# A hybrid decoder trunk in exact halves: one matmul over both halves of x in the MLP and the dilated q, k

## The chip, the cores and the metric

The kernel runs on one core of one Trainium2 chip. The metric is the device time of one execution in microseconds. A core has TensorE (PE, the matmuls; PEld is its loading of the stationary operand), VectorE (DVE), ScalarE (ACT), GpSimd (POOL) and SyncE (SP, which here issues the DMAs). The engines run their own queues in order and wait for one another on semaphores.

## What is computed

Four layers over a residual stream of 256 tokens by 1024 features, in float32. Each layer has a token mixer (a convolution module, dilated attention, RWKV-7, a convolution module), a cross-attention into 256 memory tokens, and an MLP with a squared ReLU; after each of them stands a LayerNorm.

```python
def sq_relu_mlp(x, w1, w2):
    return jnp.square(jax.nn.relu(x @ w1)) @ w2

def dilated_attention(x, w_qkv, w_out, rel_bias):
    qkv = (x @ w_qkv).reshape(b, s, n_groups, 3, DIL_HEADS, DIL_HEAD_DIM)
    for g, (win, dil) in enumerate(DIL_GROUPS):     # three groups, 16 heads of 64
        o, lse = dilated_group_attention(qkv[:, :, g, 0], qkv[:, :, g, 1], qkv[:, :, g, 2], win, dil, rel_bias)
        ...
    wts = jax.nn.softmax(jnp.stack(lses), axis=0)
    o = jnp.einsum('gbsh,gbshe->bshe', wts, jnp.stack(outs))
    return o.reshape(b, s, DIL_HEADS * DIL_HEAD_DIM).astype(x.dtype) @ w_out

def reference(x, mem, ...):
    for i in range(DEPTH):                          # 4
        h = ...                                     # conv, dilated, rwkv7, conv
        x = layer_norm(DEEPNORM_ALPHA * x + h, ln_g[i, 0], ln_b[i, 0])
        h = memory_cross_attention(x, mem, x_w_q[i], x_w_kv[i], x_w_out[i])
        x = layer_norm(DEEPNORM_ALPHA * x + h, ln_g[i, 1], ln_b[i, 1])
        h = sq_relu_mlp(x, m_w1[i], m_w2[i])        # 1024 -> 4096 -> 1024
        x = layer_norm(DEEPNORM_ALPHA * x + h, ln_g[i, 2], ln_b[i, 2])
```

## The kernel before

**Exact halves.** Every matrix product with weights is made from numbers cut in two. A number's high half is its value rounded to float32r, the low half is the rest. A product is then three matmuls into the same sum: high weights with high x, high weights with low x, low weights with high x.

**Weights.** `chunk` (L129) streams 512 KB at a time: a DMA into one of three `ws` buffers, a cast on ACT to the high half `wh` (L137), a subtraction to the low half `wl` (L138) on DVE, in places on POOL. `wh` and `wl` have nine buffers each, so a cast waits until the matmuls have finished with the chunk nine places back.

**x.** Both halves of x, transposed (features on partitions, eight blocks of 128 features, 256 tokens), lie in two tiles, `xth` and `xtl`, made by `split` (cast on ACT L151, subtraction on DVE L152).

**PSUM** has eight banks of 512 columns in three rings: A (four), B (two) and T (two, for transposes).

**MLP** (`mlp`, L399). The 4096 hidden columns are 16 units of 256. The first four are made by `first_units`; for the other twelve, `up(u)` makes a unit's hidden block with its features on partitions: `gemm_feat` runs over two halves c of 128 columns and eight blocks k of x, three matmuls of 256 tokens each (L181), 48 in all, into one bank of ring B. ACT applies Relu (L417) and Square (L418), and `split` leaves the halves `hth`, `htl`. `down(u, t)` multiplies a hidden block with its rows of w2 by `gemm_tok` (L169, 512 columns), 12 matmuls per token tile, into four A banks that are held for the whole MLP. Steps of `down(u, 0)`, `down(u, 1)`, `up(u + 5)` alternate.

**Dilated attention** (`dilated`). For each of eight pairs of heads (hp), three groups g, and q and k, `qk_unit` streams one chunk and makes 24 matmuls of 256 columns (L644) into one bank of ring B. ACT takes the sum out to the tile `qk`, scaled for q (L647), copied for k (L649). `v_units` makes the values (L193). `scores(h)` of a head makes the scores of the second token tile (L693, s1 in two A banks) and of the first (L695, s0 in a B bank); the softmax on DVE adds the biases (L673) out of PSUM, ACT takes the exponential (L679). `flip` transposes the result (L708, copies L710), `values` multiplies it with the values (L720). Scores, transposes and values of a pair are set between the next pair's `qk_unit` steps by the loop at the end of `dilated`.

**Order.** The kernel's code gives each instruction a place. A scheduler of the framework then makes one static order for each engine. At run time each engine's queue runs in that order.

**Other tiles that the change touches.** Keys and values of the cross-attention (`kv_alloc`: `kt`, `vt`, two buffers each), the memory's halves (`mem_t`), the biases and scores of the dilated attention (`hks`, `sbs`), and RWKV's `XV` and `rW` share the rings `kt`, `vt`, `xth`, `xtl`.

Of the kernel before, what the change touches and what calls it, by code (L numbers as in the profile page):

```python
# [19 lines left out]
P = 128  # L20
# [52 lines left out]
def merge(tracks):  # L73
    """Emits the steps of (generator, rank) tracks by rank; a step yields how far its track's rank moves on."""
# [9 lines left out]
class Trunk:  # L84
# [25 lines left out]
    # ---- tiles  # L110
# [61 lines left out]
    def gemm_feat(self, xt, unit, ps, toks=slice(0, S)):  # L172
        """ps[:, c, toks] = (x @ w).T of the unit's 256 columns, feature major."""
        nc = self.nc
        xh, xl = xt[0][:, :, toks], xt[1][:, :, toks]
        for c in range(2):
            for k in range(KC):
                hi, lo = unit[k // 4]
                a, b = hi[:, k % 4, c * P:(c + 1) * P], lo[:, k % 4, c * P:(c + 1) * P]
                for i, (l, r) in enumerate(((a, xh[:, k, :]), (a, xl[:, k, :]), (b, xh[:, k, :]))):  # L180
                    nc.tensor.matmul(ps[:, c * S + toks.start:c * S + toks.stop], l, r, start=k == 0 and i == 0,  # L181
                                     stop=k == KC - 1 and i == 2)
# [1162 lines left out]
```

## Time and profile before

| | |
|---|---|
| time, median of 3 executions | 2081.34 us (2080.61 to 2085.47) |
| span of the profiled execution | 2084.1 us |
| DVE busy | 1316.5 us (63%) |
| ACT busy | 998.0 us (48%) |
| POOL busy | 265.6 us (13%) |
| read from HBM | 318.81 MB, 156 GB/s over the span with the writes |
| L181: matmuls of `gemm_feat` | 3 x 1280 of 128x256 |
| L644: matmuls of `qk_unit` | 3 x 384 of 128x256 |

The profile is of one execution; no time beside its span is given for it. It lies 2.8 us above the median, within the range of the three times. The rows of a timeline give an instruction's start, its duration, engine, line, operation, tiles and shapes, and in brackets how long its engine had been idle and what released it. Rows of groups give a count, the busy time and the mean duration in ns. Durations of matmuls overlap, so the time that a matmul takes in a stream is the distance between two starts.

The page's rows of 40 slices show that PE is the busy engine nearly everywhere, with its granted clock high:

```profile
PE   7999999999999999999989989989999888999998
DVE  3986674564555557654496578777644499667454
ACT  4546455544444435455436543334645355645552
```

### The profile page before, as it was taken

To read this page: it belongs to the slowest core of one execution; us is meant where nothing else is said; L and a number is where in the kernel's file an instruction comes from. 1 tells how busy PE (TensorE), PEld (TensorE's weight loads), DVE (VectorE), ACT (ScalarE), POOL (GpSimd) and SP (SyncE) were. 2 spreads that over 40 slices of the span, in tenths; PEclk is the share of its full clock that TensorE was granted. 3 is DMA by queue.
4 is the path that set the end of the run, shared out by engine and by line. 5 is a ranking of instruction groups with operands and counts; after the bars stand their busy time and mean duration, and the time that the engine had idled before them with its cause. 6 is when DMAs were issued, how large, how long until landed. Compare 5 with 4: busy or idle time off the path is not lost.

```text
span 2084.1 us, 34386 instructions
## 1 busy us (share of the span) xinstructions
PE 1975.3 (95%) x13717; PEld 1781.3 (85%) x13717; DVE 1316.5 (63%) x2516; ACT 998.0 (48%) x1548; POOL 265.6 (13%) x160
## 2 busy tenths in 40 slices
PE   7999999999999999999989989989999888999998
PEld 7998889978989988899889878778898787888996
DVE  3986674564555557654496578777644499667454
ACT  4546455544444435455436543334645355645552
POOL 6860000000000000000021221100000663000000
PEclk8999999999999999999999989989999999999999
DMA  7644466557666635466636343433766441446652
GB/s 225 193 154 141 144 191 193 182 165 181 161 150 146 165 86 182 151 201 186 195 121 218 91 130 100 121 122 115 223 189 188 157 152 49 134 142 193 191 183 80
DMA packets 284992, 327.93 MB, mean 157 GB/s; under 512 B 25333, under 2 KB 253437, under 8 KB 284832
## 3 DMA queue, kind: packets, MB, share of 16 engines
q1 hardware_dynamic: 284832, 325.75, 52.0%
q8 instruction: 107, 1.75, 0.3%
q14 instruction: 53, 0.43, 0.1%
HBM read 318.81 MB, written 6.89 MB: 156 GB/s over the span
## 4 chain that ended last, share of the span: by engine, by line
PE 64%; DVE 14%; DMA 10%; ACT 6%; issue 3%; POOL 2%; SPq 0%; ACTq 0%; DVEq 0%; POOLq 0%
PE psA L169 20%; PE psB L181 18%; PE psB L644 6%; PE psB L193 4%; ACT wh L137 3%; DVE wl L138 3%; DVE g L535 3%; DMA ws<-in_m_w_dram 3%; PE psT L217 2%; PE psA L209 2%; POOL wl L138 2%; PE psA L193 2%; DMA ws<-in_x_w_kv_dram 2%; PE psB L370 1%; DVE bnst L267 1%
## 5 line engine op out<-in xcount | busy, mean ns | idle before, releaser
L137 ACT CAST wh<-ws 128x1024 fp32r<-128x1024 f32 x546 | 572.7, 1050 | 737.2 <-PE psA L169 197.1
L138 DVE TENSOR_TENSOR wl<-ws,wh 128x1024 fp32r<-128x1024 f32 (+1 forms) x462 | 569.5, 1234 | 415.5 <-ACT wh L137 410.9
L181 PE MATMUL psB<-xth,wh 128*128 128x256 f32 x1280 | 368.2, 288 | 8.6 <-ACT xth L151 3.6
L181 PE MATMUL psB<-xth,wl 128*128 128x256 f32 x1280 | 366.5, 286 | 7.7 <-DVE wl L138 7.7
L181 PE MATMUL psB<-xtl,wh 128*128 128x256 f32 x1280 | 367.0, 287 | 0.0
L181 PEld LDWEIGHTS psB<-xth,wh 128*128 128x128 f32 x1280 | 249.3, 195 | 12.9 <-ACT xth L151 3.8
L138 POOL TENSOR_TENSOR wl<-ws,wh 128x1024 fp32r<-128x1024 f32 x84 | 210.7, 2527 | 385.0 <-DMA ws<-in_a_w_in_dram 273.0
L181 PEld LDWEIGHTS psB<-xth,wl 128*128 128x128 f32 x1280 | 249.2, 195 | 8.9 <-DVE wl L138 8.6
L181 PEld LDWEIGHTS psB<-xtl,wh 128*128 128x128 f32 x1280 | 249.4, 195 | 2.3 <-issue 0.2
L169 PE MATMUL psA<-wh,hth 128*128 128x512 f32 x512 | 163.7, 396 | 0.0
L169 PE MATMUL psA<-wh,htl 128*128 128x512 f32 x512 | 163.3, 395 | 0.0
L169 PE MATMUL psA<-wl,hth 128*128 128x512 f32 x512 | 162.2, 393 | 0.0
L209 PE MATMUL psA<-wh,xth 128*128 128x256 f32 x512 | 145.7, 285 | 0.0
L209 PE MATMUL psA<-wh,xtl 128*128 128x256 f32 x512 | 145.4, 287 | 0.2 <-DVE xtl L152 0.2
L209 PE MATMUL psA<-wl,xth 128*128 128x256 f32 x512 | 144.5, 283 | 0.0
L535 DVE SCALAR_TENSOR_TENSOR psA<-chp,ccols,psA 128x256 f32<-128x256 f32 x280 | 119.1, 482 | 3.0 <-PE psA L519 0.4
L644 PE MATMUL psB<-xth,wh 128*128 128x256 f32 x384 | 112.6, 293 | 6.4 <-ACT qk L647 4.6
L169 PEld LDWEIGHTS psA<-wl,hth 128*128 128x128 f32 x512 | 96.5, 188 | 22.9
L169 PEld LDWEIGHTS psA<-wh,htl 128*128 128x128 f32 x512 | 96.2, 188 | 22.0
L844 POOL MEMSET rH<- 128x512 f32 x1 | 0.5, 527 | 894.0 <-DVE bnst L267 894.0
L644 PE MATMUL psB<-xtl,wh 128*128 128x256 f32 x384 | 110.5, 288 | 0.0
L644 PE MATMUL psB<-xth,wl 128*128 128x256 f32 x384 | 110.1, 287 | 0.0
(327 smaller groups left out, 3994.3 us busy)
## 6 DMA issues: line engine op xcount, KB each, us to landing
ws<-in_m_w_dram SPq DMA_DIRECT2D x256, 512.0 KB, 3.8
ws<-in_b_w_qkv_dram SPq DMA_DIRECT2D x72, 512.0 KB, 3.8
ws<-in_x_w_kv_dram SPq DMA_DIRECT2D x64, 512.0 KB, 3.6
ws<-in_a_w_in_dram SPq DMA_DIRECT2D x32, 512.0 KB, 4.5
ws<-in_x_w_q_dram SPq DMA_DIRECT2D x32, 512.0 KB, 4.3
ws<-in_x_w_out_dram SPq DMA_DIRECT2D x32, 512.0 KB, 3.9
ws<-in_c_w_rkv_dram SPq DMA_DIRECT2D x24, 512.0 KB, 4.4
ws<-in_a_w_out_dram SPq DMA_DIRECT2D x16, 512.0 KB, 3.3
```

The source lines that it names most:

```text
L137: nc.scalar.copy(out=h[:rows], in_=f[:rows])
L138: self.lo_eng.tensor_tensor(l[:rows], f[:rows], h.bitcast(F32)[:rows], op=OP.subtract)
L169: nc.tensor.matmul(ps[j], l, r[:, j * 512:(j + 1) * 512], start=first and k == 0 and i == 0, stop=last and k == n - 1 and i == 2)
L181: nc.tensor.matmul(ps[:, c * S + toks.start:c * S + toks.stop], l, r, start=k == 0 and i == 0, stop=k == KC - 1 and i == 2)
L193: nc.tensor.matmul(ps[:, m * 256:(m + 1) * 256], l, r[:, k % 4, :], start=k == 0 and i == 0, stop=k == KC - 1 and i == 2)
L209: nc.tensor.matmul(out[-1][:, o], l, r[:, k % 4, :], start=k == 0 and i == 0, stop=k == KC - 1 and i == 2)
L217: self.pe_last = self.nc.tensor.transpose(pt[:, i * P:(i + 1) * P], b, self.ident).ins
L267: v.bn_stats(st[:, j, :], xs)
L370: nc.tensor.matmul(op[:, c * S:(c + 1) * S], vt[:, m, (2 * h + c) * P:(2 * h + c + 1) * P], pT[:, m, :], start=m == 0, stop=m == 1)
L535: v.scalar_tensor_tensor(dst[:, o], hp[:, c, k:k + S], dwc(k, cc), src[:, o], op0=OP.mult, op1=OP.add)
L644: nc.tensor.matmul(ps, l[:, k, :], r[:, k, :], start=k == 0 and i == 0, stop=k == KC - 1 and i == 2)
L844: nc.gpsimd.memset(H, 0.0)
```

## The change

1. **One tile for both halves of x.** `halves` allocates x's high and low parts in one tile, [128, 8, 2, 256], so that for each block k the 512 columns [high | low] are contiguous.
2. **`feat2`** replaces `gemm_feat` in the MLP's `up` and the three matmuls in `qk_unit`. For each block k it makes one matmul of 512 columns with the high weights, over both halves of x, into a whole bank of ring B, and one of 256 columns with the low weights and high x, into the left half of that bank. Three matmuls and three weight loads become two and two. In the MLP each half c of a unit has a bank of its own.
3. **The eviction** adds the bank's halves: ACT copies (or scales) the right half to SBUF, DVE adds the left half to it (in `qk_unit` with q's scale). In the MLP Relu then reads SBUF.
4. **Rings.** `xth` and `xtl` become one ring `xt`, `kt` and `vt` one ring `kv`, with two buffers each; all tiles in them are merged pairs. RWKV's W of both token tiles is one tile. Comments are removed, and line numbers move.

`gemm_feat` stays for the cross-attention, the convolutions and RWKV.

```diff
+    def halves(self, tag, name):
+        x = self.sb.tile([P, KC, 2, S], F32R, name=name, tag=tag, bufs=2)
+        return x[:, :, 0, :], x[:, :, 1, :], x
+
     def xt(self):
-        h = self.sb.tile([P, KC, S], F32R, name="xth", tag="xth", bufs=2)
-        l = self.sb.tile([P, KC, S], F32R, name="xtl", tag="xtl", bufs=2)
-        return h, l
+        return self.halves("xt", "xt")
...
+    def feat2(self, xt, w):
+        nc = self.nc
+        ps = self.B()
+        for k in range(KC):
+            a, b = w(k)
+            nc.tensor.matmul(ps, a, xt[2][:, k].rearrange("p a b -> p (a b)"), start=k == 0, stop=k == KC - 1,
+                             skip_group_check=True)
+            nc.tensor.matmul(ps[:, :S], b, xt[0][:, k, :], start=False, stop=k == KC - 1, skip_group_check=True)
+        return ps
...
     def kv_alloc(self):
-        kt = self.sb.tile([P, KC, S], F32, name="kt", tag="kt", bufs=2)
-        vt = self.sb.tile([P, NT, D], F32, name="vt", tag="vt", bufs=2)
-        return kt, vt
+        kv = self.sb.tile([P, 2, 2048], F32, name="kv", tag="kv", bufs=2)
+        return kv[:, 0].rearrange("p (a b) -> p a b", b=S), kv[:, 1].rearrange("p (a b) -> p a b", b=D)
...
         def up(u):
-            ps = self.B()
-            self.gemm_feat(xt, self.colunit(w1, u * 256), ps)
+            unit = self.colunit(w1, u * 256)
             r = self.g2()
-            nc.scalar.activation(r, ps, AF.Relu)
+            for c in range(2):
+                ps = self.feat2(xt, lambda k: [a[:, k % 4, c * P:(c + 1) * P] for a in unit[k // 4]])
+                o = r[:, c * S:(c + 1) * S]
+                nc.scalar.copy(out=o, in_=ps[:, S:])
+                nc.vector.tensor_tensor(o, o, ps[:, :S], op=OP.add)
+            nc.scalar.activation(r, r, AF.Relu)
             nc.scalar.activation(r, r, AF.Square)
             self.split(*hidden(u), r.rearrange("p (a b) -> p a b", a=2))
...
-        hks = self.sb.tile([P, 2, 4, S], F32, name="hks", tag="kt", bufs=2)
-        sbs = self.sb.tile([P, 2, 1024], F32, name="sbs", tag="vt", bufs=2)
+        hs = self.sb.tile([P, 2, 2, 1024], F32, name="hs", tag="kv", bufs=2)
+        hks, sbs = hs[:, 0].rearrange("p a (b c) -> p a b c", c=S), hs[:, 1]
...
         def qk_unit(hp, g, c):
-            ps = self.B()[:, :S]
-            for k in range(KC):
-                for i, (l, r) in enumerate(((hi, xt[0]), (hi, xt[1]), (lo, xt[0]))):
-                    nc.tensor.matmul(ps, l[:, k, :], r[:, k, :], start=k == 0 and i == 0, stop=k == KC - 1 and i == 2)
+            ps = self.feat2(xt, lambda k: (hi[:, k, :], lo[:, k, :]))
             o = qk[hp, g, c] = dp.tile([P, S], F32, name="qk", bufs=12)
-            if c == 0:
-                nc.scalar.mul(out=o, in_=ps, mul=DE ** -0.5)
-            else:
-                nc.scalar.copy(out=o, in_=ps)
+            sc = DE ** -0.5 if c == 0 else 1.0
+            nc.scalar.mul(out=o, in_=ps[:, S:], mul=sc)
+            v.scalar_tensor_tensor(o, ps[:, :S], sc, o, op0=OP.mult, op1=OP.add)
...
-            W = st["W", t] = self.sb.tile([P, NH, 2, 2, P], F32, name="rW", bufs=2,
-                                            tag=(("kt", "vt") if hq != 2 else ("xth", "xtl"))[t])
+            if t == 0:
+                st["WW"] = self.sb.tile([P, NT, NH, 2, 2, P], F32, name="rW", bufs=2, tag="kv" if hq != 2 else "xt")
+            W = st["W", t] = st["WW"][:, t]
```

**Where the instructions stand.** In the MLP, on PE at the beginning of a unit: the last matmuls of a down product (psA), then the first of the unit (psB). Before:

```order
L169 MATMUL psA_3283<-wh_3360,htl_3030 128x512
L169 MATMUL psA_3284<-wh_3360,htl_3030 128x512
L181 MATMUL psB_3389<-xth_2338,wh_3391 128x256
L181 MATMUL psB_3389<-xtl_2339,wh_3391 128x256
L181 MATMUL psB_3389<-xth_2338,wl_3392 128x256
```

and of the changed kernel, on the same engine at the same place:

```order
L172 MATMUL psA_3274<-wh_3340,htl_3021 128x512
L172 MATMUL psA_3275<-wh_3340,htl_3021 128x512
L195 MATMUL psB_3382<-xt_2332,wh_3370 128x512
L197 MATMUL psB_3382<-xt_2332,wl_3371 128x256
L195 MATMUL psB_3382<-xt_2332,wh_3370 128x512
```

The unit keeps its place between the down products; three matmuls of a block have become two.

In the dilated attention, on PE around the scores of an even head, whose newest k has just been made (in the trace near 580.8 us). Before:

```order
L644 MATMUL psB_5920<-xth_2972,wl_5916 128x256
L708 MATMUL psT_5982<-ident_72,sbs_4787 128x128 x2
L693 MATMUL psA_5949<-qk_5945,qk_5912 128x256
L695 MATMUL psB_5950<-qk_5669,qk_5607 128x128
L695 MATMUL psB_5950<-qk_5816,qk_5783 128x128
L695 MATMUL psB_5950<-qk_5945,qk_5912 128x128
L693 MATMUL psA_6076<-qk_5669,qk_5607 128x256
L693 MATMUL psA_6076<-qk_5816,qk_5783 128x256
L644 MATMUL psB_6000<-xth_2972,wh_5995 128x256
```

and of the changed kernel, where the scores have the lines L708 (before L693) and L710 (before L695):

```order
L195 MATMUL psB_5657<-xt_2964,wh_5652 128x512
L197 MATMUL psB_5657<-xt_2964,wl_5653 128x256
L708 MATMUL psA_5679<-qk_5674,qk_5648 128x256
L710 MATMUL psB_5680<-qk_5426,qk_5371 128x128
L710 MATMUL psB_5680<-qk_5559,qk_5533 128x128
L710 MATMUL psB_5680<-qk_5674,qk_5648 128x128
L708 MATMUL psA_5792<-qk_5426,qk_5371 128x256
L708 MATMUL psA_5792<-qk_5559,qk_5533 128x256
L195 MATMUL psB_5730<-xt_2964,wh_5725 128x512
```

The scores with the newest k, qk_5674, now follow its unit directly; the two transposes have moved ahead of the unit.

On DVE at the same place, before (wl are weights' low halves for later units, dmx and sbs belong to the softmax of these scores):

```order
L673 ISA sbs_4787,dmx_5958<-psA_5948,hks_4786 128x512
L673 ISA dmx_5958 128x1
L138 TENSOR_TENSOR wl_6309<-ws_6307,wh_6308 128x1024
L138 TENSOR_TENSOR wl_6381<-ws_6379,wh_6380 128x1024
L673 ISA sbs_4787,dmx_5960<-psA_5949,hks_4786,dmx_5958 128x256
```

and of the changed kernel, where L664 is the new addition to qk, and the subtraction's line is L141:

```order
L688 ISA hs_4644,dmx_5688<-psA_5678,hs_4644 128x512
L688 ISA dmx_5688 128x1
L664 SCALAR_TENSOR_TENSOR qk_5648<-psB_5631,qk_5648 128x256
L141 TENSOR_TENSOR wl_5997<-ws_5995,wh_5996 128x1024
L141 TENSOR_TENSOR wl_6069<-ws_6067,wh_6068 128x1024
L664 SCALAR_TENSOR_TENSOR qk_5674<-psB_5657,qk_5674 128x256
L688 ISA hs_4644,dmx_5690<-psA_5679,hs_4644,dmx_5688 128x256
```

The addition that completes the newest k, qk_5674, stands behind two weight subtractions, the second of which (wl_6069) has the place of wl_6381 before. On ACT the cast of that chunk stands ahead of the copy of qk in both kernels.

More of the change, by code (lines that the diff above doesn't have):

```diff
@@ L157, in gemm_tok @@
         nc = self.nc
-        xh, xl = xt
+        xh, xl = xt[:2]
         n = len(ws)
@@ L170, in gemm_tok, with gemm_feat, feat @@
                                      start=first and k == 0 and i == 0, stop=last and k == n - 1 and i == 2)
-    def gemm_feat(self, xt, unit, ps, toks=slice(0, S)):
+    def gemm_feat(self, xt, unit, ps):
+        for c in range(2):
+            self.feat(ps[:, c * S:(c + 1) * S], xt, lambda k: [a[:, k % 4, c * P:(c + 1) * P] for a in unit[k // 4]])
+    def feat(self, ps, xt, w):
         nc = self.nc
-        xh, xl = xt[0][:, :, toks], xt[1][:, :, toks]
-        for c in range(2):
-            for k in range(KC):
[L178 to L182, printed above, removed]
+        for k in range(KC):
+            a, b = w(k)
+            for i, (l, r) in enumerate(((a, xt[0]), (a, xt[1]), (b, xt[0]))):
+                nc.tensor.matmul(ps, l, r[:, k, :], start=k == 0 and i == 0, stop=k == KC - 1 and i == 2)
+    def feat2(self, xt, w):
+        nc = self.nc
+        ps = self.B()
+        for k in range(KC):
+            a, b = w(k)
+            nc.tensor.matmul(ps, a, xt[2][:, k].rearrange("p a b -> p (a b)"), start=k == 0, stop=k == KC - 1,
+                             skip_group_check=True)
+            nc.tensor.matmul(ps[:, :S], b, xt[0][:, k, :], start=False, stop=k == KC - 1, skip_group_check=True)
+        return ps
     def gemm_unit(self, xt, unit, ps, tiles=(0, 1)):
         nc = self.nc
-        xh, xl = xt
+        xh, xl = xt[:2]
         for m in tiles:
@@ L198, in first_units @@
         nc = self.nc
-        xh, xl = xt
+        xh, xl = xt[:2]
         out = []
@@ L220, in to_xt @@
     def to_xt(self, xt, src, t):
-        xh, xl = xt
+        xh, xl = xt[:2]
         for q in range(2):
@@ L289, in mem_t @@
         if spare:
-            mt = (self.sb.tile([P, KC, S], F32R, name="mth", tag="kt", bufs=2),
-                  self.sb.tile([P, KC, S], F32R, name="mtl", tag="vt", bufs=2))
+            mt = self.halves("kv", "mt")
         elif pool is None:
@@ L294, in mem_t @@
         else:
-            mt = pool.tile([P, KC, S], F32R, name="mth"), pool.tile([P, KC, S], F32R, name="mtl")
+            mt = pool.tile([P, KC, 2, S], F32R, name="mt")
+            mt = mt[:, :, 0, :], mt[:, :, 1, :], mt
         for m in range(NT):
@@ L413, in up @@
         def up(u):
-            ps = self.B()
-            self.gemm_feat(xt, self.colunit(w1, u * 256), ps)
+            unit = self.colunit(w1, u * 256)
             r = self.g2()
-            nc.scalar.activation(r, ps, AF.Relu)
+            for c in range(2):
+                ps = self.feat2(xt, lambda k: [a[:, k % 4, c * P:(c + 1) * P] for a in unit[k // 4]])
[3 more added lines that the diff above has]
+            nc.scalar.activation(r, r, AF.Relu)
             nc.scalar.activation(r, r, AF.Square)
@@ L612, in dil_table @@
         nc.sync.dma_start(rb[:BUCKETS, :], t_["rel_bias"])
-        oh = self.sb.tile([P, G, TW], F32, name="onehot", tag="kt", bufs=2)
+        oh = self.sb.tile([P, G, TW], F32, name="onehot", tag="kv", bufs=2)
         nc.sync.dma_start(oh[:BUCKETS + 1], t_["rel_onehot"])
@@ L640, in qk_unit @@
             hi, lo = self.chunk(w[:, c0:c0 + P].rearrange("(k p) n -> p k n", p=P), (KC, P))
-            ps = self.B()[:, :S]
-            for k in range(KC):
-                for i, (l, r) in enumerate(((hi, xt[0]), (hi, xt[1]), (lo, xt[0]))):
-                    nc.tensor.matmul(ps, l[:, k, :], r[:, k, :], start=k == 0 and i == 0, stop=k == KC - 1 and i == 2)
+            ps = self.feat2(xt, lambda k: (hi[:, k, :], lo[:, k, :]))
             o = qk[hp, g, c] = dp.tile([P, S], F32, name="qk", bufs=12)
-            if c == 0:
-                nc.scalar.mul(out=o, in_=ps, mul=DE ** -0.5)
-            else:
-                nc.scalar.copy(out=o, in_=ps)
+            sc = DE ** -0.5 if c == 0 else 1.0
+            nc.scalar.mul(out=o, in_=ps[:, S:], mul=sc)
+            v.scalar_tensor_tensor(o, ps[:, :S], sc, o, op0=OP.mult, op1=OP.add)
         def v_units(hq, gs):
@@ L816, in rwkv @@
         XK, XR = self.xt(), self.xt()
-        XV = (self.sb.tile([P, KC, S], F32R, name="xvh", tag="kt", bufs=2),
-              self.sb.tile([P, KC, S], F32R, name="xvl", tag="vt", bufs=2))
+        XV = self.halves("kv", "xv")
         def mixes(m, dst):
```

## The prediction

> **What bounds the kernel now.** I read the page's busy lines first, then its chain, then a table of stretches.
>
> ```profile
> span 2084.1 us, 34386 instructions
> ...
> PE 1975.3 (95%) x13717; PEld 1781.3 (85%) x13717; DVE 1316.5 (63%) x2516; ACT 998.0 (48%) x1548; POOL 265.6 (13%) x160
> ...
> PE 64%; DVE 14%; DMA 10%; ACT 6%; issue 3%; POOL 2%; SPq 0%; ACTq 0%; DVEq 0%; POOLq 0%
> PE psA L169 20%; PE psB L181 18%; PE psB L644 6%; PE psB L193 4%; ACT wh L137 3%; DVE wl L138 3%; DVE g L535 3%; DMA ws<-in_m_w_dram 3%; PE psT L217 2%; PE psA L209 2%; POOL wl L138 2%; PE psA L193 2%; DMA ws<-in_x_w_kv_dram 2%; PE psB L370 1%; DVE bnst L267 1%
> ```
>
> TensorE is busy 95% of the span, and the two lines that the change rewrites, L181 and L644, hold 24% of the chain that ended last. The stretches to look at are one MLP (308 to 433 us) and the dilated attention (487 to 755 us).
>
> ```profile
> 308.00:433.00 125.00, 125.00 (x796) 113.31 (x795) 62.72 (x56) 66.78 (x80) 0.00 (x0) 1.00 0.61 190
> 487.00:755.00 268.00, 258.11 (x2028) 242.57 (x2027) 138.36 (x269) 120.51 (x202) 0.00 (x0) 0.98 0.64 160
> ```
>
> The columns are the stretch, its length, busy time of PE, PEld, DVE, ACT and POOL with counts, granted clock, DMA share and GB/s. In the MLP PE never pauses (125.00 of 125.00, clock 1.00), while DVE and ACT work half of the time and the DMA engines 0.61. There a shorter PE stream shortens the stretch, and DVE and ACT have room. The dilated stretch already has 9.9 us without matmuls: there PE sometimes waits for others.
>
> **The matmuls saved.** A matmul's recorded duration overlaps its successor, so I count the time from start to start.
>
> ```profile
> 351.23 0.28 PE L181 MATMUL psB<-xtl,wh 128*128 128x256 f32 x1
> ...
> 352.43 0.28 PE L181 MATMUL psB<-xth,wl 128*128 128x256 f32 x1
> 352.55 0.62 PE L169 MATMUL psA<-wh,hth 128*128 128x512 f32 x2
> ...
> 355.33 0.64 PE L169 MATMUL psA<-wh,hth 128*128 128x512 f32 x2
> ...
> 262.67 0.62 PE L169 MATMUL psA<-wl,xth 128*128 128x512 f32 x2
> ...
> 267.65 0.61 PE L169 MATMUL psA<-wh,xth 128*128 128x512 f32 x2
> ```
>
> From 351.23 to 352.43 ten 256-column matmuls of the MLP start: 120 ns each (119.8 over the stretch). Of 512 columns, six pairs from 352.55 to 355.33 give 232 ns each, and eleven pairs of a projection, from 262.67 to 267.65, give 226 to 227. So two 256-column matmuls cost 239.6, one of 512 columns 227 to 232: the join saves 12.6 ns, or 7.5. I take 12.8 (two of 119.8 less 226.8), because the stationary side is again a block of 128 columns and the moving side one contiguous row of 512, as in the projection. Joined are 768 groups in the MLP (48 units by up, of 2 halves and 8 blocks each) and 384 in the dilated attention (48 units of 8): 768 x 12.8 ns = 9.8 us and 384 x 12.8 ns = 4.9 us, **14.7 us** together; 8.6 by the other row.
>
> The Trainium skill, "TensorE: Matmul & The Clock Gate", section "Back-to-back issue gap", speaks against this: it puts the fixed part of a warm matmul's spacing at about 2.5 ns. By that a join would save 2.5 ns, 2.9 us in all (an estimate from that page). The rows disagree: 120 and 227 ns fit a fixed part near 13 ns.
>
> **The new eviction in the MLP.** A unit's one Relu out of PSUM becomes two copies on ACT, two adds on DVE, and a Relu out of SBUF.
>
> ```profile
> L417 ACT ACTIVATE g<-psB x12: 587/588/593, 308.2 to 432.9; 128x512 f32<-128x512 f32 x12
> ...
> L647 ACT ACTIVATE qk<-psB 128x256 f32<-128x256 f32 x24 | 9.1, 378 | 0.1
> ...
> L649 ACT COPY qk<-psB 128x256 f32<-128x256 f32 x24 | 8.7, 364 | 0.0
> ...
> L137 ACT CAST wh<-ws 128x1024 fp32r<-128x1024 f32 x69 | 72.2, 1047 | 115.9 <-issue 53.9 <-PE psB L644 31.5 <-DMA ws<-in_b_w_qkv_dram 20.7
> ...
> L138 DVE TENSOR_TENSOR wl<-ws,wh 128x1024 fp32r<-128x1024 f32 x68 | 83.2, 1223 | 78.0 <-ACT wh L137 77.6
> ...
> L535 DVE SCALAR_TENSOR_TENSOR psA<-chp,ccols,psA 128x256 f32<-128x256 f32 x280 | 119.1, 482 | 3.0 <-PE psA L519 0.4
> ...
> L152 DVE TENSOR_TENSOR xtl<-psB,xth 128x256 fp32r<-128x256 f32 x6 | 2.5, 418 | 0.0
> ```
>
> The Relu rows span 308.2 to 432.9, twelve of them, so a step takes 11.33 us. Into it come two ACT copies of 0.37 (L649) and two DVE adds between 0.42 (L152) and 0.48 (L535). ACT goes from 66.8/125 to about 60% busy, DVE from 50 to 59%. Neither reaches PE. A half's bank must be back when the unit after next begins: the down products of 24 matmuls, 24 x 0.232 = 5.6 us, lie between two units, and even behind a cast (1.05) and a weight subtraction (1.22) the eviction takes 0.1 + 1.05 + 0.37 + 1.22 + 0.48 = 3.2 us. So it costs nothing; without that cover it would be 0.5 to 3.2 us per unit. The hidden block comes some 0.8 us later to its down products, which are units away. The MLP's term is **-9.8**, and its bounds are -5.8 and, if the join saved nothing, 0.
>
> **The new eviction in the dilated attention.** Here the newest q or k is needed at once. The place is that of the two order listings:
>
> ```profile
> 580.82 0.29 PE L644 MATMUL psB<-xth,wl 128*128 128x256 f32 x1
> ...
> 580.95 0.38 PE L708 MATMUL psT<-ident,sbs 128*128 128x128 f32 x2
> 581.06 1.04 ACT L137 CAST wh<-ws 128x1024 fp32r<-128x1024 f32 x1 [3.18 <-PE psB L644]
> 582.01 0.37 ACT L649 COPY qk<-psB 128x256 f32<-128x256 f32 x1
> 582.14 1.23 DVE L138 TENSOR_TENSOR wl<-ws,wh 128x1024 fp32r<-128x1024 f32 x1 [2.62 <-ACT wh L137]
> ...
> 582.43 0.70 PE L693 MATMUL psA<-qk 64*128 64x256 f32 x2 [1.11 <-ACT qk L649]
> ```
>
> The unit ends at 580.94. Its end frees the weight buffer for which ACT's cast has waited, the cast goes first, the copy ends at 582.38, and PE's scores L693 have waited 1.11 us. In the new DVE order the add stands behind the wl subtraction that this cast releases. That runs to 582.14 + 1.23 = 583.37, and the add, 0.48, to 583.85. PE's scores then start near 583.9: 1.47 us later. Behind the waiting scores are queued the first-half scores, the next unit's matmuls, and on DVE the softmax; none of these can go ahead, so the whole 1.47 us is on the path. This place comes three times (three waits of up to 1.1 in the grouped rows below; the second is at 654.63): 4.4 us.
>
> ```profile
> 594.44 0.93 PE L695 MATMUL psB<-qk 64*128 64x128 f32 x6
> ...
> 595.85 0.39 PE L644 MATMUL psB<-xth,wh 128*128 128x256 f32 x1 [0.47 <-ACT qk L649]
> ...
> 498.28 0.58 PE L644 MATMUL psB<-xth,wh 128*128 128x256 f32 x1 [4.61 <-ACT qk L647]
> ...
> PE psB L644 <- ACT qk L647: 4.6, 1, 4.6
> PE psA L693 <- ACT qk L649: 3.3, 3, 1.1
> PE psB L644 <- ACT qk L649: 1.4, 3, 0.5
> ```
>
> The last three rows group PE's waits for q and k: us in total, times, longest.
>
> At 595.85 a unit waits 0.47 us (one of three) for its bank, which the copy (L649) returns. Now the add returns it, right behind the copy: 0.48 later, three times, 1.4 us. At the first pair's start (498.28 waits for q, too) one add more is 0.5. Elsewhere the bank or the q comes back E + 2.95 us after a unit's end E (the sum at 580.94: 583.85 + 0.04), where before it was E + 1.44. At four places the scores have about 2.6 us of other matmuls ahead of them: 0.35 each, 1.4. Where units follow one another directly, the bank is wanted after one joined unit, 8 x (0.227 + 0.120) = 2.78: about 0.15 each at 13 of the units, 2.0. The waits sum to 4.4 + 1.4 + 0.5 + 1.4 + 2.0 = **+9.7**. The bounds are 0 (all adds early) and 48 x 0.48 = 23 (every add in the way).
>
> **The clock.** Waits cost twice when the granted clock falls behind them.
>
> ```profile
> 1748.54 0.30 PE L217 MATMUL psT<-ident,g 128*128 128x128 f32 x1 [1.93 <-DVE g L535]
> ...
> 1058.67 0.63 PE L217 MATMUL psT<-ident,x 128*128 128x128 f32 x4 [1.90 <-DVE x L273]
> ...
> 654.63 0.70 PE L693 MATMUL psA<-qk 64*128 64x256 f32 x2 [1.11 <-ACT qk L649]
> ...
> 656.90:660.30 3.40, 3.40 (x18) 3.40 (x18) 2.63 (x9) 1.42 (x4) 0.00 (x0) 0.50 0.88 204
> 584.50:587.90 3.40, 3.40 (x28) 3.27 (x28) 2.81 (x9) 1.65 (x5) 0.00 (x0) 1.00 0.87 218
> 1749.30:1752.70 3.40, 3.40 (x19) 3.40 (x18) 3.40 (x10) 0.00 (x0) 0.00 (x0) 0.51 0.00 0
> 1059.80:1063.20 3.40, 3.40 (x18) 3.40 (x18) 3.24 (x12) 0.12 (x1) 0.05 (x1) 0.51 0.00 0
> ```
>
> Behind the pauses of 1.93 and 1.90 us PE runs 3.4 us at 0.50 to 0.51 of its clock, as behind all 16 pauses that long. Behind the equal pauses of 1.11 us it did so once (656.90) and not at 584.50. Such a stretch does 1.7 us of work in 3.4: it costs 1.7. The three pauses grow from 1.11 to 2.6, so two of them should gain such a stretch: **+3.4**, between 0 and, with the smaller new waits, 7.
>
> The Trainium skill, same page, section "HAM oscillation — how this bites in real kernels", wants pauses of more than about 3.4 us before the clock falls. The rows with 1.9 and 1.11 disagree. By that rule the sum would be 3.4 us lower.
>
> **The merged tiles.** x's two halves become one tile, and the keys, values, biases and RWKV's W share one ring. In the order almost nothing moves outside the two stages, and what a merged tile waits for, the later of two releases, comes well before its use where I followed it. I take 0, within 3 us either way (an estimate, from the spread of the three runs, 2080.61 to 2085.47).
>
> **Sum.** -9.8 - 4.9 + 9.7 + 3.4 = -1.6 us. The profiled execution's span of 2084.1 would become 2082.5; it lies 2.8 above the median of 2081.34, which becomes **2079.7**.
>
> **The rivals.** (1) *The waits are hidden*: the adds, ready a little earlier or later than the order suggests, find DVE free. For it speaks that DVE is busy only 138 of 268 us; against it, that DVE takes its work in order and sits behind the very cast. Then 2.5 us of waits stay and no clock falls: 2081.3 - 14.7 + 2.5 = 2069.1. (2) *The clock does not fall*: the longer pauses behave like the one before 584.50. The sum without 3.4: 2076.3. (3) *Slower: the add is in the way at every q, k unit.* Its price is 0.48 at each of 48 units, 23.0 us, and 3.4 for the clock, against 14.7: 2093.0. It decides from 14.7/48 = 0.31 us per unit. For it speaks that the banks B are two and one of them goes to scores; against it, that PE waited for q and k at only seven places (1 + 3 + 3). (4) *Slower: the join saves nothing*, so that a 512-column matmul beside a 256-column one costs the 239.6 ns of two: 2081.3 + 13.1 = 2094.4. The two rows of 227 and 232 speak against it, though none alternates the two widths. By the skill's figure above it would be 2.9 less.
>
> **How the numbers follow.** Chances: the forecast 0.38, rival (1) 0.22, (2) 0.15, (3) 0.15, (4) 0.10. A measurement can tell some 0.3%, 6.2 us, from no change: 2075.1 to 2087.6. The forecast with its small terms (8.6 instead of 14.7; the tiles' 3) falls below 2075.1 one time in ten, above 2087.6 about as rarely; (1) is nearly always faster; (2) lies at the bound and is faster one time in three; (3) and (4) are slower. Faster: 0.04 + 0.20 + 0.05 = 0.29; slower: 0.02 + 0.15 + 0.09 = 0.26; within: 0.45. The range takes in rival (1) and reaches to (3): 2068 to 2093. The forecast's own range is 2073 to 2087.
>
> **What would show it.** Pairs of one 512- and one 256-column matmul 347 ns apart (before 359 for three); the MLP's step 11.13 instead of 11.33 us, with PE still unbroken; in the dilated attention three PE pauses near 2.6 us released by DVE's qk add, and a clock of 0.50 behind them; the stage about 8 us longer, the four MLPs together about 10 shorter. Pairs 359 apart would make the first term wrong, pauses that stay near 1.1 us the second. A prediction of no change is wrong if one of these two terms is off by more than 6 us.

## The result and the profile after

The change made the kernel slower: **2103.3 us** (median of 6 executions, 2097.1 to 2107.4) against 2081.2 before, a ratio of 1.0107 with a 95% interval of 1.009 to 1.0125. Timed once more beside before on another occasion it took 2099.7 us, ratio 1.0094 (1.0076 to 1.0113). The profiled execution has a span of 2105.1 us.

The page of the changed kernel, with the engines' busy time and the chain that ended last:

```profile
span 2105.1 us, 32339 instructions
...
PE 1974.4 (94%) x12565; PEld 1721.5 (82%) x12565; DVE 1366.9 (65%) x2660; ACT 1032.0 (49%) x1644; POOL 262.7 (12%) x160
...
PE 40%; DVE 14%; DMA 5%; ACT 3%; issue 2%; POOL 0%; DVEq 0%; ACTq 0%; SPq 0%; POOLq 0%
...
L195 PE MATMUL psB<-xt,wh 128*128 128x512 f32 x1152 | 418.9, 405 | 7.8 <-DVE qk L664 5.8
L197 PE MATMUL psB<-xt,wl 128*128 128x256 f32 x1152 | 326.0, 283 | 0.0
```

1152 matmuls fewer, as the change says, and PE is as long busy as before (1974.4 for 1975.3 us). Recorded durations of matmuls overlap, and at half clock each takes longer (a 256-column matmul at 587.46 us 0.56 us, at full clock 0.28), so this sum alone tells neither where time was saved nor where it was lost. The chain's shares sum to 64% here and to 99% in the page before, so the two chains are not compared. Cut at the LayerNorms, the two profiled executions show where the time went: the four MLPs together are 4.6 us shorter (by their own lengths -1.7, -0.1, -1.5 and -1.3), the dilated attention with its LayerNorm is 17.5 us longer (456.6 to 792.7 for 459.6 to 778.2), RWKV with the cross-attention behind it 5.8, and the second layer's cross-attention 3.0.

The dilated stage, in the table of stretches, with PE's grouped waits in it:

```profile
456.60:792.70 336.10, 311.77 (x1942) 264.16 (x1942) 184.38 (x387) 136.75 (x229) 0.00 (x0) 0.95 0.58 142
...
PE psA L708 <- DVE qk L664: 8.7, 4, 2.7
PE psB L195 <- DVE qk L664: 5.8, 5, 4.4
PE psB L735 <- DVE dnm L693: 3.8, 3, 1.3
PE psB L195 <- DVE dmx L688: 2.0, 3, 0.7
```

In the stretch's row stand PE, PEld, DVE, ACT, POOL, then the clock: 0.95. PE now waits for DVE's addition to q and k (L664) where it waited for ACT's copy. All waits of the stage, these and two more of 4.1 us together at its beginning, are 24.4 us for 13.1 before.

The place whose order rows are shown above, from the timeline of the changed kernel:

```profile
580.49 0.28 PE L197 MATMUL psB<-xt,wl 128*128 128x256 f32 x1
580.73 1.04 ACT L140 CAST wh<-ws 128x1024 fp32r<-128x1024 f32 x1 [3.95 <-PE psB L195]
581.68 0.38 ACT L663 ACTIVATE qk<-psB 128x256 f32<-128x256 f32 x1
581.81 1.23 DVE L141 TENSOR_TENSOR wl<-ws,wh 128x1024 fp32r<-128x1024 f32 x1 [3.05 <-ACT wh L140]
582.95 0.42 DVE L664 SCALAR_TENSOR_TENSOR qk<-psB,qk 128x256 f32<-128x256 f32 x1
583.42 0.70 PE L708 MATMUL psA<-qk 64*128 64x256 f32 x2 [2.66 <-DVE qk L664]
...
590.95 0.38 PE L723 MATMUL psT<-ident,hs 128*128 128x128 f32 x2
...
592.43 0.42 DVE L664 SCALAR_TENSOR_TENSOR qk<-psB,qk 128x256 f32<-128x256 f32 x1
...
592.77 0.14 DVE L693 TENSOR_SCALAR dnm<-dmx 128x1 f32<-128x1 f32 x1
592.90 1.30 PE L735 MATMUL psB<-g,vv 128*64 128x256 f32 x12 [1.25 <-DVE dnm L693]
```

Read from top to bottom: the unit ends, the cast runs, the copy follows it, the cast's own subtraction on DVE is released before the copy is done, the addition stands behind it, and PE waits 2.66 us. Ten microseconds later comes a wait that the prediction did not have: PE's products with the values (L735) wait 1.25 us. Their row names the softmax's step dnm, but in the trace dnm ended 4 to 8 ns after PE had started, here and at all twelve such places in the four profiles that have three each; the addition ended 53 to 55 ns before it, as the other addition did before 583.42 (0.05 us). The code agrees: `values` takes a bank of ring B, which the addition has to return, and does not read dnm. This addition, too, stands behind a weight subtraction. In the kernel before, ACT's copy returned the bank, and the row of the products shows no wait:

```profile
588.83 0.38 ACT L647 ACTIVATE qk<-psB 128x256 f32<-128x256 f32 x1
588.99 1.22 DVE L138 TENSOR_TENSOR wl<-ws,wh 128x1024 fp32r<-128x1024 f32 x1
589.27 1.93 PEld L720 LDWEIGHTS psB<-g,vv 128*64 128x64 f32 x24 [0.17 <-ACT qk L647]
589.27 2.17 PE L720 MATMUL psB<-g,vv 128*64 128x256 f32 x24
```

Both places come three times.

The clock behind the three long pauses:

```profile
584.70:588.10 3.40, 3.40 (x12) 2.43 (x10) 2.90 (x11) 2.00 (x5) 0.00 (x0) 0.50 0.77 177
659.80:666.60 6.80, 6.25 (x22) 4.94 (x23) 4.20 (x16) 2.10 (x5) 0.00 (x0) 0.50 0.48 106
738.30:745.10 6.80, 6.44 (x22) 5.14 (x23) 4.20 (x15) 2.10 (x5) 0.00 (x0) 0.50 0.51 109
```

At all three the clock falls to half, twice for 6.8 us; there it fell 0.4 to 0.6 us before the pause had ended. In the whole stage half clock lasts 30.7 us for 17.1 before.

In the MLP the matmuls stand like this in the changed kernel:

```profile
348.88 0.40 PE L195 MATMUL psB<-xt,wh 128*128 128x512 f32 x1
349.12 0.28 PE L197 MATMUL psB<-xt,wl 128*128 128x256 f32 x1
349.23 0.40 PE L195 MATMUL psB<-xt,wh 128*128 128x512 f32 x1
...
349.94 0.40 PE L195 MATMUL psB<-xt,wh 128*128 128x512 f32 x1
350.18 0.28 PE L197 MATMUL psB<-xt,wl 128*128 128x256 f32 x1
350.30 0.62 PE L172 MATMUL psA<-wh,hth 128*128 128x512 f32 x2
...
L437 ACT ACTIVATE g<-g x12: 631/631/632, 309.6 to 432.2; 128x512 f32<-128x512 f32 x12
```

From 348.88 to 349.94 are three pairs: 353 ns each, for three matmuls of 120 before, so a join saves 6 ns. A step of the MLP takes (432.2 - 309.6)/11 = 11.15 us (median over all four MLPs 11.21, before 11.33).

### The profile page after: what moved, and what is told of

Read it like the earlier page. It is cut to its first block, busy times and chain, and to the rows that moved or that the text cites. A ratio compares the mean times of both kernels' runs of the same rounds, so it can differ in the third digit from the quotient of the medians.

```text
span 2105.1 us, 32339 instructions
## 1 busy us (share of the span) xinstructions
PE 1974.4 (94%) x12565; PEld 1721.5 (82%) x12565; DVE 1366.9 (65%) x2660; ACT 1032.0 (49%) x1644; POOL 262.7 (12%) x160
## 4 chain that ended last, share of the span: by engine, by line
PE 40%; DVE 14%; DMA 5%; ACT 3%; issue 2%; POOL 0%; DVEq 0%; ACTq 0%; SPq 0%; POOLq 0%
PE psA L172 15%; PE psB L195 7%; PE psB L197 4%; DVE g L554 3%; PE psB L186 3%; DVE wl L141 3%; PE psA L225 2%; PE psT L233 2%; DMA ws<-in_m_w_dram 2%; ACT wh L140 1%; DVE psA L554 1%; PE psB L385 1%; DVE bnst L283 1%; DVE x L288 1%; DMA ws<-in_x_w_out_dram 1%
## 5 line engine op out<-in xcount | busy, mean ns | idle before, releaser
L141 DVE TENSOR_TENSOR wl<-ws,wh 128x1024 fp32r<-128x1024 f32 (+1 forms) x462 | 566.2, 1233 | 269.7 <-ACT wh L140 264.5
L195 PE MATMUL psB<-xt,wh 128*128 128x512 f32 x1152 | 418.9, 405 | 7.8 <-DVE qk L664 5.8
L197 PE MATMUL psB<-xt,wl 128*128 128x256 f32 x1152 | 326.0, 283 | 0.0
L195 PEld LDWEIGHTS psB<-xt,wh 128*128 128x128 f32 x1152 | 219.5, 191 | 65.0 <-DVE qk L664 7.5
L141 POOL TENSOR_TENSOR wl<-ws,wh 128x1024 fp32r<-128x1024 f32 x84 | 210.5, 2533 | 388.2 <-ACT wh L140 375.0
L197 PEld LDWEIGHTS psB<-xt,wl 128*128 128x128 f32 x1152 | 220.5, 191 | 1.7
L186 PE MATMUL psB<-xt,wh 128*128 128x256 f32 x1024 | 196.4, 293 | 10.5 <-ACT xt L154 3.6
L225 PE MATMUL psA<-wh,xt 128*128 128x256 f32 x1024 | 193.7, 287 | 0.0
L186 PEld LDWEIGHTS psB<-xt,wh 128*128 128x128 f32 x1024 | 166.8, 200 | 13.7 <-ACT xt L154 4.2
L225 PEld LDWEIGHTS psA<-wh,xt 128*128 128x128 f32 x1024 | 162.5, 193 | 0.5 <-ACT xt L154 0.2
L186 PE MATMUL psB<-xt,wl 128*128 128x256 f32 x512 | 149.1, 291 | 7.7 <-DVE wl L141 7.7
L172 PE MATMUL psA<-wh,xt 128*128 128x512 f32 x512 | 155.0, 403 | 1.3 <-ACT xt L154 1.3
L225 PE MATMUL psA<-wl,xt 128*128 128x256 f32 x512 | 145.3, 284 | 0.0
L172 PEld LDWEIGHTS psA<-wh,xt 128*128 128x128 f32 x512 | 96.6, 191 | 22.3 <-ACT xt L154 2.6
```

The costliest lines, as they stand in the source:

```text
L141: self.lo_eng.tensor_tensor(l[:rows], f[:rows], h.bitcast(F32)[:rows], op=OP.subtract)
L172: nc.tensor.matmul(ps[j], l, r[:, j * 512:(j + 1) * 512], start=first and k == 0 and i == 0, stop=last and k == n - 1 and i == 2)
L186: nc.tensor.matmul(ps, l, r[:, k, :], start=k == 0 and i == 0, stop=k == KC - 1 and i == 2)
L195: nc.tensor.matmul(ps, a, xt[2][:, k].rearrange("p a b -> p (a b)"), start=k == 0, stop=k == KC - 1, skip_group_check=True)
L197: nc.tensor.matmul(ps[:, :S], b, xt[0][:, k, :], start=False, stop=k == KC - 1, skip_group_check=True)
L225: nc.tensor.matmul(out[-1][:, o], l, r[:, k % 4, :], start=k == 0 and i == 0, stop=k == KC - 1 and i == 2)
```

## The experiments

Times are medians; ratios are to before, run beside them. In these groups of runs before took 2081.8, 2080.7, 2080.0 and 2080.3 us. A profile shows one execution, which need not lie at the median: that of the merged tiles alone took 2081.7 us for a median of 2086.4, the first kernel with all improvements 2079.7 for 2086.4, the kernel before with the one edit 2080.1 for 2074.1. So causes are read from waits and distances in the profiles, and gains from the medians.

### The tiles alone, and the join in one stage alone

Three kernels keep the merged tiles. The first has all products and evictions as before, the second joins in the MLP alone, the third in q and k alone:

```diff
-            ps = self.feat2(xt, lambda k: (hi[:, k, :], lo[:, k, :]))
+            ps = self.B()[:, :S]
+            self.feat(ps, xt, lambda k: (hi[:, k, :], lo[:, k, :]))
...
-                ps = self.feat2(xt, lambda k: [a[:, k % 4, c * P:(c + 1) * P] for a in unit[k // 4]])
...
+            self.gemm_feat(xt, self.colunit(w1, u * 256), ps)
```

> Only the merged tiles: all products as before, in three matmuls of 256 columns, and the old evictions. Theory A (the prediction's term of 0: the rings cost nothing): 2081 us, within 3. Theory B (the merged tiles change the order at the end of the RWKV stage, where the changed kernel has two pauses of PE of over 6 us, 6.35 and 6.22, for one of 7.32 before): about 5.5 us more, 2085 to 2089, with both pauses of over 6 us in the trace.

> Merged tiles and the joined matmul in the MLP alone; q and k as before. Against the run with the merged tiles alone: theory A (the prediction's price, 12.8 ns saved per join): 9.8 us less. Theory B (the changed kernel's own rows: a 512- and a 256-column matmul together 353 to 355 ns for three at 359, so 5 ns saved per join): 4 to 5 us less. Theory C (the join saves nothing): the same.

> Merged tiles and the joined matmul with its new eviction in q and k alone; the MLP as before. Against the run with the merged tiles alone: theory A (the prediction's terms: -4.9 for the joins, 9.7 of waits, 3.4 of clock): 8 us more. Theory B (the account of the changed kernel's trace: waits of 12 us, 9 of half clock, 2 to 5 saved, and up to 3 behind the stage): 17 to 20 us more.

Merged tiles alone: 2086.4, ratio 1.003 (1.0017 to 1.0043), 4.5 us over before. Join in the MLP: 2080.0, ratio 0.9995 (0.9979 to 1.0012), 6.4 below the tiles alone. Join in q and k: 2103.4, ratio 1.0109 (1.0079 to 1.0139), 17.0 over the tiles alone. So the tiles are not free, the MLP gains half to two thirds of the predicted 9.8 us (4.6 by the distances, 768 x 6.0 ns, and by the lengths of the four MLPs), and most of the loss lies in q and k.

What the tiles do is seen at the end of RWKV, in PE's rows that waited, with the tiles merged:

```profile
1359.74 0.69 PE L233 MATMUL psT<-ident,g 128*128 128x128 f32 x2 [6.35 <-DVE g L1146]
...
1376.73 1.94 PE L233 MATMUL psT<-ident,x 128*128 128x128 f32 x8 [6.41 <-DVE x L289]
...
PE psT L233 <- DVE x L289: 8.5, 3, 6.4
...
PE psT L233 <- DVE g L1146: 6.4, 1, 6.4
```

PE waits there first for the gate's output and then for the LayerNorm of both token tiles. Before, the first tile's LayerNorm fell into the wait for the second tile's gate.

### Which ring it is

```diff
-        kv = self.sb.tile([P, 2, 2048], F32, name="kv", tag="kv", bufs=2)
+        kt = self.sb.tile([P, KC, S], F32, name="kt", tag="kt", bufs=2)
+        vt = self.sb.tile([P, NT, D], F32, name="vt", tag="vt", bufs=2)
...
+            if hq != 2:
+                W = st["W", t] = self.sb.tile([P, NH, 2, 2, P], F32, name="rW", bufs=2, tag=("kt", "vt")[t])
```

> Only x's halves (and the W that lies in their ring) in one tile; keys, values, biases, memory and the other W in two rings as before; products and evictions as before. Theory A (what the merged tiles cost comes from the merged ring of keys and values, by which the order at the end of RWKV changes): the order there is as before, one pause of over 6 us instead of two, and the time is that of before, 2082 within 2. Theory B (it comes from x's merged tile): 4 to 5 us more than before, as with both merged.

2080.7 us, ratio 1.0004 (0.9989 to 1.0019): the cost is gone. PE's rows at the same place, with the keys' and values' rings as before:

```profile
1352.53 0.44 PE L233 MATMUL psT<-ident,g 128*128 128x128 f32 x2 [1.37 <-DVE g L1152]
...
1363.77 0.69 PE L233 MATMUL psT<-ident,g 128*128 128x128 f32 x2 [7.32 <-DVE g L1152]
...
PE psT L233 <- DVE g L1152: 8.7, 2, 7.3
...
PE psT L233 <- DVE x L289: 2.1, 2, 1.9
```

One long pause instead of two. The last two rows of each fence sum PE's waits from 1040 to 1400 us: for these two together 14.9 us with the merged ring and 10.8 with two rings, 4.1 apart for 4.5 in the times. In all profiles with the merged ring, nine of them, PE waits 34.1 to 35.4 us from the layer's start to the LayerNorm behind RWKV, in the five with two rings 27.7 to 31.5. So it is the ring of keys, values and RWKV's W, not x's merged tile. That the ring acts through the scheduler's order is read from these rows; it was not tested apart.

### Grouping the two widths in the MLP

```diff
         for k in range(KC):
-            a, b = w(k)
-            nc.tensor.matmul(ps, a, xt[2][:, k].rearrange("p a b -> p (a b)"), start=k == 0, stop=k == KC - 1,
+            nc.tensor.matmul(ps, w(k)[0], xt[2][:, k].rearrange("p a b -> p (a b)"), start=k == 0, stop=k == KC - 1,
                              skip_group_check=True)
-            nc.tensor.matmul(ps[:, :S], b, xt[0][:, k, :], start=False, stop=k == KC - 1, skip_group_check=True)
+        for k in range(KC):
+            nc.tensor.matmul(ps[:, :S], w(k)[1], xt[0][:, k, :], start=False, stop=k == KC - 1, skip_group_check=True)
```

> As the joined matmul in the MLP alone, but the eight matmuls of 512 columns come first and the eight of 256 columns after them. Theory A (the loss against the prediction comes from the alternation of the two widths): 512-column matmuls 227 to 232 ns apart, 256-column ones 120, and 3 to 5 us less than with the alternating order. Theory B (a 512-column matmul that moves both halves of x takes 236 ns by itself): the same time as with the alternating order, and 236 ns between the 512-column matmuls.

2075.9 us, ratio 0.998 (0.9965 to 0.9994), 4.1 below the alternating order. The eight wide matmuls of a half unit in its timeline:

```profile
353.46 2.01 PE L194 MATMUL psB<-xt,wh 128*128 128x512 f32 x8
355.31 0.88 PE L197 MATMUL psB<-xt,wl 128*128 128x256 f32 x6
```

Eight take 1.85 us to the next start, 231 ns each, and the narrow ones are 119 ns apart: 351 ns for a pair. Over all pairs of starts at full clock the means are 231.9 and 118.9 grouped, 236.5 and 116.9 alternating (the run with the join in the MLP alone). Theory A holds, but a wide matmul that moves x costs what the one of the down product costs (232), not what the one of the projection costs (227). A join then saves 8.6 ns. By these distances the grouping is worth 768 x 2.6 ns = 2.0 us of the 4.1; the rest is within the intervals of the two ratios.

### The eviction without the join, and on other engines

Three edits, one for each run: the new eviction with three matmuls; the join with the eviction on DVE alone; the change's eviction with the subtractions on POOL:

```diff
-            nc.tensor.matmul(ps, a, xt[2][:, k].rearrange("p a b -> p (a b)"), start=k == 0, stop=k == KC - 1,
-                             skip_group_check=True)
+            nc.tensor.matmul(ps[:, :S], a, xt[0][:, k, :], start=k == 0, stop=k == KC - 1, skip_group_check=True)
+            nc.tensor.matmul(ps[:, S:], a, xt[1][:, k, :], start=False, stop=k == KC - 1, skip_group_check=True)
...
-            nc.scalar.mul(out=o, in_=ps[:, S:], mul=sc)
+            v.tensor_scalar(o, ps[:, S:], sc, None, op0=OP.mult)
             v.scalar_tensor_tensor(o, ps[:, :S], sc, o, op0=OP.mult, op1=OP.add)
...
         w = t_["b_w_qkv"][j]
+        self.lo_eng = nc.gpsimd
```

> Merged tiles; q and k with the new eviction, but no joined matmul: high weights with x's high half and with its low half are two matmuls of 256 columns into the two halves of the bank. The MLP as before. Theory A (the eviction alone makes the dilated attention longer, and the join gives back 2 to 3 us): 2 to 3 us over the run with the join in q and k, 19 to 20 over the merged tiles alone, with the same pauses of 2.66 and 1.25 us. Theory B (the join itself does harm there, for instance by 512-column matmuls that wait for x's low half or slow the clock): 5 us or more below the run with the join.

> Merged tiles; q and k joined as in the change, but the eviction stands on DVE alone: DVE scales the right half into SBUF and adds the left half to it, ACT does nothing for it. More work on DVE, less on ACT. Theory A (the harm comes from the chain cast, copy, weight subtraction, addition: the addition waits in DVE's queue behind a subtraction that is released earlier): the pauses of 2.66 us fall to 1 us or less, the half clock behind them goes, the dilated attention takes 312 to 320 us for 335.6, and the time is 0 to 6 us below the merged tiles alone. Theory B (the harm is the additional work on DVE or the longer hold of the bank): the stage stays above 328 us.

> As the joined q and k with the change's eviction, but in the dilated attention the weight subtractions stand on POOL (2.5 us each instead of 1.2), so that only the additions and the softmax are left on DVE. Theory A (the place behind the subtraction is the harm): the addition follows the copy at once, the pauses of 2.66 us become 1.6, at most one in three is followed by half clock, and the stage takes 322 to 328 us for 335.6; POOL's longer subtractions may take some of it back. Theory B (DVE's load is not what delays the addition): pauses of 2.6 us and a stage of 333 us or more.

Three matmuls: 2105.1, ratio 1.0128 (1.0102 to 1.0153), and the same pauses of 2.65 and 1.25. The loss is the eviction's; what the join gives back, 1.7 us, is less than the intervals can tell.

DVE alone: 2080.7, ratio 0.9996 (0.9982 to 1.001), 5.7 below the tiles alone and 22.7 below the same matmuls with the change's eviction. The stage and its waits for q and k:

```profile
456.20:769.40 313.20, 299.91 (x1942) 259.18 (x1941) 203.87 (x434) 122.27 (x181) 0.00 (x0) 0.98 0.61 152
...
PE psB L195 <- DVE qk L660: 6.0, 4, 5.4
PE psA L704 <- DVE qk L660: 1.9, 4, 0.5
```

DVE is busier (203.9 for 184.4 us in the changed kernel's stage) and the stage 23 us shorter. More work on DVE was not the harm. What this run takes away is the wait behind ACT's cast and copy and behind the subtraction that the cast releases: both steps of the eviction now stand ahead of that subtraction, and the longest pause at the newest k is 0.5 us.

POOL: 2099.9, ratio 1.009 (1.0063 to 1.0118), 3.5 below the run with the change's eviction; the stage takes 332.8 us, so the expected 322 to 328 was not reached. Two of the three pauses fell to 1.80, a little over the 1.6 expected, but all three were still followed by half clock, which lasts 27.3 us in the stage as in the run with the change's eviction. The third place is a control within the run: its subtraction belongs to the output weights and stood on DVE.

```profile
586.82 0.70 PE L705 MATMUL psA<-qk 64*128 64x256 f32 x2 [1.80 <-DVE qk L661]
...
734.86 1.04 ACT L140 CAST wh<-ws 128x1024 fp32r<-128x1024 f32 x1 [3.94 <-PE psB L195]
735.81 0.38 ACT L660 ACTIVATE qk<-psB 128x256 f32<-128x256 f32 x1
735.93 1.23 DVE L141 TENSOR_TENSOR wl<-ws,wh 128x1024 fp32r<-128x1024 f32 x1 [3.04 <-ACT wh L140]
737.08 0.41 DVE L661 SCALAR_TENSOR_TENSOR qk<-psB,qk 128x256 f32<-128x256 f32 x1
...
737.55 0.70 PE L705 MATMUL psA<-qk 64*128 64x256 f32 x2 [2.65 <-DVE qk L661]
```

There the pause is 2.65 as in the changed kernel. Side by side the runs give the parts of a pause: 0.5 us with both steps on DVE, 1.11 behind cast and copy (before), 1.80 with the addition behind them, 2.65 with the subtraction ahead of the addition. So the subtraction is 0.85 us of it, and to take it away was not enough. How much time POOL's slower subtractions (2.4 us in the median) cost elsewhere in this run was not measured apart: all waits of the stage are 23.2 us for 24.4 in the changed kernel.

### All improvements together, a miss, and its repair

The first kernel groups the widths everywhere, evicts q and k on DVE and keeps the keys' and values' rings apart. The changed kernel ran beside it.

> The joined matmul in the MLP and in q and k, with the eight 512-column matmuls ahead of the eight of 256; q's and k's eviction on DVE alone; only x's halves (and the W in their ring) in a merged tile, keys and values in two rings as before. If the parts add up: 0 for the tiles, 10 us saved in the MLP (the grouped run against the merged tiles), 6 in the dilated attention by the DVE eviction and up to 3 by the grouping there: 2063 to 2068 us, 13 to 18 below before. If the kernel is bound by something that the parts share, or if the grouping delays the eviction's start in q and k: 2070 or more.

> The changed kernel once more beside before on one chip. If its parts add up: 2081 + 4.5 (tiles) - 6.4 (MLP) + 17 (q and k) = 2096 to 2098 us. If they disturb one another: 2102 or more, as the first median of 2103.3 says.

2086.4 us, ratio 1.0025 (1.001 to 1.004): about 20 us off the expectation. The dilated stage took 325.3 us, and the rows of DVE and PE at the known place show why:

```profile
572.27 0.42 DVE L665 TENSOR_SCALAR qk<-psB 128x256 f32<-128x256 f32 x1 [2.61 <-PE psB L197]
572.62 1.21 DVE L141 TENSOR_TENSOR wl<-ws,wh 128x1024 fp32r<-128x1024 f32 x1
573.75 0.41 DVE L666 SCALAR_TENSOR_TENSOR qk<-psB,qk 128x256 f32<-128x256 f32 x1
574.22 0.70 PE L710 MATMUL psA<-qk 64*128 64x256 f32 x2 [1.98 <-DVE qk L666]
```

With the wide matmuls first, the high weights are done with a microsecond before the unit ends. The next cast starts earlier, and its subtraction comes between the eviction's two steps: pauses of 1.98 us. The changed kernel, run again, took 2099.7 us; the parts (4.5 - 6.4 + 17.0) had given 2096 to 2098.

The repair groups in the MLP alone (`grouped` is true there, false for q and k). A last run puts the old, single eviction of q and k on DVE in the kernel before:

```diff
-            if c == 0:
-                nc.scalar.mul(out=o, in_=ps, mul=DE ** -0.5)
-            else:
-                nc.scalar.copy(out=o, in_=ps)
+            v.tensor_scalar(o, ps, DE ** -0.5 if c == 0 else 1.0, None, op0=OP.mult)
```

> As the kernel before this one (joined everywhere, DVE eviction of q and k, keys and values in two rings), but the 512-column matmuls are grouped ahead of the 256-column ones in the MLP alone; in q and k they alternate. Theory A (in that kernel the grouping freed a weight buffer before the unit's end, so that the next cast and its subtraction came between the eviction's two steps on DVE: pauses of 1.98 us): the subtraction no longer comes between, the pauses of PE in the dilated attention fall below 0.7 us, the stage takes 312 to 315 us for 325.3, and the time is 2064 to 2070 us. Theory B (the loss there comes from the two rings or from something that MLP and q, k share): stage above 320 us and 2075 us or more.

> The kernel before with one edit: q's and k's single eviction is a DVE multiplication instead of ACT's copy; no join, no merged tiles. Theory A (the gain of the DVE eviction is that it doesn't stand behind ACT's cast, and the join adds only 2 to 3 us to it): the three pauses of 1.11 us go, the dilated attention takes 314 to 317 us for 318.7, and the time is 2 to 5 us below before. Theory B (the gain came with the join): the same time as before.

The repaired kernel takes **2067.6 us**, ratio 0.9937 (0.9923 to 0.9951), its dilated stage 311.1 us. The kernel before with the one edit takes 2074.1, ratio 0.9966 (0.9953 to 0.998), its stage 312.6 us: 6.2 below before, more than the expected 2 to 5. So in q and k the gain is where the eviction stands: with the join and a DVE eviction the stage took 311.1 and 313.2 us, without the join 312.6, each with 13.7 us of half clock.

## Why the prediction was wrong

It forecast 2079.7 in 2068 to 2093; 2103.3 lies outside. The place of the harm and its first cause were right. What failed is the sum: it left out the bank that the products with the values need, put the tiles at nothing, and mis-sized the joins and the clock. By its own steps:

- **The MLP's join, -9.8.** Measured 6.4 less by the medians, 4.6 by the distances. The term was mis-sized: it took the projection's 226.8 ns for the wide matmul, where the alternating stream showed 236.5 + 116.9. Its own lower row, 232, gave 5.8. That the eviction costs nothing there was right: PE stays unbroken (125.00 of the 125 us from 308 to 433) and the step is shorter. By the 2.5 ns of the Trainium skill ("TensorE: Matmul & The Clock Gate", "Back-to-back issue gap"), which that section gives for an isolated matmul and not for a stream of weight loads and matmuls as here, a join would have saved 2.5 ns; the rows show 6.0 alternating and 8.6 grouped.
- **The join in q and k, -4.9.** It has the same price: 384 x 6.0 ns = 2.3 us by the distances. With and without it the runs differ by 1.7, within their intervals.
- **The waits at the newest k, 4.4.** Right in mechanism and size. The pauses rose from 1.11 to 2.66, and the rows stand in the order that was worked out: cast, copy, subtraction, addition.
- **The other waits, 5.3.** All waits of the stage rose by 11.3 us (24.4 for 13.1) for 9.7 in the sum, but the near match is in part luck. The sum had the late bank for the next unit alone (0.48 each, the addition right behind the copy). Missing were the products with the values, which take a bank as soon as a unit is done: 3.8 us in three waits, with the addition behind a subtraction there, too. The units' own waits (L195), priced at 1.4 + 0.5 + 2.0, rose from 6.0 to 7.8 us.
- **The clock, +3.4.** The step that counted one stretch of 3.4 us for two of the pauses failed. Two pauses brought 6.8 us, the third 3.4, and in the stage 13.6 us more ran at half clock, which costs 6.8. It also varies: in the repeated run of the same kernel two of three pauses had such a stretch, half clock in the stage was 20.5 us, 3.4 more than before, and the stage took 329.6 us for 336.1. In the four profiles with pauses of 2.66 the three together brought 17.0, 6.8, 17.0 and 10.2 us. The premise, that a pause of 1.9 us is always followed by half clock as in the one profile before, does not hold in the others (last section).
- **The tiles, 0 within 3.** Wrong: 4.5. The prediction had checked when the buffers come free, and took the order outside the two stages as almost unmoved. It had moved at the end of RWKV, and this decided whether one token tile's LayerNorm lies under another wait.
- **Sum.** Measured apart, the parts are the MLP's -6.4, +17.0 for q and k (forecast -4.9 + 9.7 + 3.4 = +8.2) and +4.5 for the tiles: 15.1 us for the forecast's -1.6. That explains 2096 of the 2099.7 and 2103.3. What the remaining 3 to 7 us are stays open; the 3.0 us in the second layer's cross-attention, with a half clock of its own, did not come again in the repeated run.

Rival (3), the slower one, had its place and sign right (the addition in the way), though not at every unit: a few places, each with its clock behind it, cost 11.3 + 6.8 = 18.1 us in the profile, for its 23.0 + 3.4. That its 2093 and rival (4)'s 2094.4 lay nearest to the measured time is luck: (3) had 14.7 for the joins and nothing for the tiles, and in (4) the joins save nothing, where they do save 6.0 ns each. Rival (2) speaks for longer pauses that leave the clock alone, and the trace spoke against it, as it does against the Trainium skill's "TensorE: Matmul & The Clock Gate", section "HAM oscillation — how this bites in real kernels", which asks for pauses of more than about 3.4 us: 16 of the 18 pauses between 1.8 and 2.7 us at this place, over the profiles of six runs, were followed by half clock. The pauses of 1.1 us, in the kernel before and four others, were so in 3 of 15.

## What to carry to other kernels

Splitting an eviction over two engines can put its second half behind whatever the first engine's earlier work releases on the second; read the order of both queues, and all that stands behind the new instruction, before counting its half microsecond. An eviction that is needed at once belongs, in this kernel, whole on one engine that isn't at that moment given a longer instruction by the same event. Ask not only who reads the result but who takes the bank next. Merging tiles changes when buffers come free and can so change the scheduler's order far from the edit: such shuffles are part of the change and have to be priced.

## What the hardware showed

A 512-column matmul followed by one of 256 columns takes 236.5 ns to the next start and the other 116.9; eight of one width in a row take 231.9 and 118.9 each. Why the alternation costs 2.6 ns a pair is not settled. At the newest k, pauses of 1.8 to 2.0 us were followed by a half clock of 3.4 us in each of five cases. Elsewhere the same length is not enough: the pause of 1.9 us at the LayerNorm in front of RWKV (between 1044 and 1076 us), which all fourteen profiles have, was followed by it in nine and not in five.

Half clock begins on a grid. In each of the fourteen profiles all its starts lie whole numbers of 3.413 us apart, to 1 or 2 ns (584.7, 659.8 and 738.3 above are 22 and 23 steps apart), and it lasts one to four steps, except for the last stretch, at the program's end. Where that pause of 1.9 us lay whole inside one step, in eight profiles, half clock followed each time; where a step's border cut it, in six, once. So a pause's place on the grid counts beside its length, which fits the different stretches behind equal pauses above. It is not the whole rule: at the newest k cut pauses of 1.8 to 2.7 us were followed more often than not.
